# Two of the four weight chunks of the first layer's output product as groups of seven products of sums

## The chip, the cores and the metric

The kernel runs on one core of a Trainium2 chip. The metric is the time of one launch on the device in microseconds (us), the median of several runs. The core has five engines that run side by side, each with its own queue: TensorE (PE in the profile; its weight loads stand apart as PEld), VectorE (DVE), ScalarE (ACT), GpSimd (POOL) and SyncE (SP, which here only starts transfers). They wait for each other by semaphores.

## What is computed

A block of two layers over 528 tokens (16 meta tokens and 512 of the input) with 1024 channels, all in float32. What matters here is how a layer ends and how the next begins:

```python
def hybrid_layer(x, norm_g, w_in, ..., w_a, w_b, w_out, cos, sin, k_top):
    h = rms_norm(x, norm_g)
    proj = jnp.einsum('btd,de->bte', h, w_in)
    ...
    y_a = jnp.einsum('bte,ed->btd', attn * jax.nn.silu(gate_a), w_a)
    ...
    y_b = jnp.einsum('bte,ed->btd', pooled * jax.nn.silu(gate_b), w_b)
    g_a, g_b = jnp.split(jax.nn.sigmoid(merge), 2, axis=-1)
    return x + jnp.einsum('btd,de->bte', g_a * y_a + g_b * y_b, w_out)
```

The last line is the output product: a 528 x 1024 matrix of merged activations by the 1024 x 1024 matrix `w_out`. Its result is the next layer's input `x`, and the next layer starts with the sum of squares over the channels of each token (`rms_norm`).

## The kernel before

**Precision.** TensorE takes its operands as `F32R` (a rounded float32). To keep more digits, every operand is split into a high part (a cast by ACT) and a rest (value minus high part, a subtraction by DVE or POOL), and a product is made in three passes that accumulate in one PSUM bank: high by high, high by rest, rest by high. Activations lie transposed: channels in the 128 partitions (eight blocks, index `k` or `j`), tokens along the free axis.

**Weights.** `chunks` lists pieces of the weight matrices in the order of use, 27 per layer; the last four of a layer are 256 columns of `w_out` each (numbers 23 to 26 in the first layer), and before them stand the two chunks of `w_a` (21, 22). SP loads a chunk into two `raw` buffers; four such buffers are there, two chunks at a time, and `w_load` starts the next load where a chunk's buffers come free. The splitting is cut into items in `prep_q`; `group_done`, called after every group of matmuls, runs one item. There are three kinds. Plain chunks: two casts of 1024 elements by ACT and two subtractions by DVE. Chunks in `by_dma`: the rest is made by ACT (minus the value, rounded) and a transfer from POOL's queue that adds the value onto it, so that DVE has nothing to do; then the two casts. Chunks in `mixed`: see below.

**Groups of seven products.** `group_of_products` multiplies a chunk of 256 columns, seen as 2 x 2 blocks (input channels halved, output channels halved), by activations seen as 2 x 2 blocks (channels halved, tokens halved), with seven block products in place of eight. `mixed_prep` makes the seven left operands of a chunk in nine items (four blocks and three sums `s1`, `s2`, `s3`/`s4` of blocks, each with a high part and a rest; two of the sums are made by accumulating transfers on POOL's queue, `first_sum` and the one from `s2` onto `a12`). The seven right operands are four sums and three plain blocks. Each product is 12 matmuls. Three PSUM banks serve a group; `out` copies a bank to a sheet (ACT), `total` adds a bank and a sheet (DVE), `direct` takes a bank. Before the change the groups serve the ten `mixed` chunks of `w_in` in each layer (`mix_gates`), and the last two chunks of `w_out` in the second layer only (`mix_out`, with right operands from `sums_of_merged`).

**The end of the first layer.** Chunks 21 and 22 (`w_a`) are multiplied in eight channel blocks `j`, each in two token parts (272 and 256 tokens) of 12 matmuls. After each part DVE finishes `ta[j]` with two instructions, ACT casts it to `hhi`, and POOL makes the rest `hlo` (DVE does for `j` = 7). Then `out_group` makes one block of 128 output channels for one token part: 24 matmuls of a dense product, one DVE instruction that adds half the result to the residual `RES`, ACT's square, and POOL's addition of the square to `sq`. Chunks 23 and 24 run over both token parts. Chunks 25 and 26 are held together: first both for tokens 0 to 271, then both for tokens 272 to 527. Between the second token part's four blocks stand `stats(0)` (sums of squares of the first token part, on TensorE) and `norm_half(1, 0, ...)` (its normalization for the second layer). The second layer begins with `plain_trio`, which reads `NF[0]` of the first token part, block after block.

**Order.** PE and DVE follow the order of the code. ACT, POOL and SP are put in order by the framework's scheduler; `issue_after` sets a lower bound for some. `later(fn, n)` runs `fn` n groups later; `group_done` calls `half_done`, and `dense` also calls one of them halfway through a block.

The names the steps below use: `chunks`, `mixed`, `by_dma`, `SOFT`, `first_sum`, `mixed_prep` (items `i0` to `i8`), `half_done`, `group_of_products`, `ROLES`, `NEEDS`, `LEAD`, `sums_of_merged`, `out_group`, `stats`, `norm_half`.

## Time and profile before

| | us |
|---|---|
| median of 3 runs (735.25 to 736.46) | 735.64 |
| the profiled execution | 736.32 |
| its span, first to last instruction | 734.5 |
| chunks 21 and 22 (`w_a`, first layer) | from about 305.9 to 329.3 |
| output product of the first layer | 329.3 to 378.0 |

The span is split by the profile into instructions of each engine. A matmul's end is modelled and matmuls overlap, so the pitch, the distance from one start to the next, is what a matmul costs; the durations (near 0.28 us) are longer than the pitch. "Idle before" an instruction names who ended the wait. A busy PE is therefore read from gaps and pitches, not from the busy share. Every line that the argument uses is shown in the prediction.

### The profile page before, as it was taken

How to read it: one execution, taken by the hardware profiler on the slowest of the kernel's cores; microseconds unless marked ns; L12 is line 12 of the kernel's file. 1: busy time of each engine (PE TensorE's matmuls, PEld its weight loads, DVE VectorE, ACT ScalarE, POOL GpSimd, SP SyncE). 2: the span in 40 equal slices, each digit the busy share in tenths (PEclk: the TensorE clock that was granted, in tenths of full speed). 3: DMA queues.
4: the chain of work that ended last, by engine and by line, in shares of the span. 5: the costliest groups of instructions: out<-in, count | busy, mean ns of one | idle time of the engine just before them, and what ended most of it. 6: DMA issues, size and time to landing. Idle time of an engine off the chain costs nothing.

```text
span 734.5 us, 16031 instructions
## 1 busy us (share of the span) xinstructions
PE 726.9 (99%) x5917; PEld 701.1 (95%) x5917; DVE 589.4 (80%) x1480; ACT 487.2 (66%) x1109; POOL 254.6 (35%) x337
## 2 busy tenths in 40 slices
PE   8999999999999999999999999999999999999998
PEld 8999999999999999999999989999899999999997
DVE  6776899999997776794358668999989978668774
ACT  6669735766789887543245696357588978775643
POOL 3652174731221211173247421757132222106300
PEclk9999999999999999999999999999999999999999
DMA  8766675874564434633422678649565654447832
GB/s 268 234 172 155 164 159 116 216 160 101 119 141 115 90 87 113 209 125 126 136 89 87 172 170 203 159 116 200 131 153 107 143 113 93 114 140 237 202 88 72
DMA packets 103566, 106.41 MB, mean 145 GB/s; under 512 B 5008, under 2 KB 83632, under 8 KB 103488
## 3 DMA queue, kind: packets, MB, share of 16 engines
q1 hardware_dynamic: 91888, 74.89, 33.4%
q0 software_dynamic: 11520, 30.41, 23.3%
q8 instruction: 46, 0.75, 0.4%
q14 instruction: 32, 0.26, 0.1%
q10 hardware_dynamic: 80, 0.08, 0.0%
HBM read 66.41 MB, written 8.55 MB: 102 GB/s over the span
## 4 chain that ended last, share of the span: by engine, by line
PE 90%; DVE 4%; DMA 2%; ACT 2%; issue 1%; POOL 1%; SPq 1%; DVEq 0%; POOLq 0%; ACTq 0%
PE d L63 73%; PE a L63 12%; PE v L63 4%; DMA xt<-in_x_dram 2%; DVE w L63 1%; DVE alo L63 0%; SPq L156 0%; DVE c L63 0%; SPq L434 0%; DVE sila L63 0%; ACT w L225 0%; DVE t L63 0%; ACT w L269 0%; POOL t L683 0%; ACT lt L800 0%
## 5 line engine op out<-in xcount | busy, mean ns | idle before, releaser
L63 PE MATMUL d<-hhi,w 128*128 128x256 f32 (+3 forms) x1392 | 278.8, 291 | 0.3 <-DVE c L63 0.3
L63 PEld LDWEIGHTS d<-hhi,w 128*128 128x128 f32 x1392 | 222.2, 188 | 3.8 <-DVE c L63 0.7
L63 PE MATMUL d<-hlo,w 128*128 128x256 f32 (+3 forms) x696 | 189.8, 288 | 0.0
L63 DVE TENSOR_TENSOR w<-raw,w 128x512 fp32r<-128x512 f32 (+1 forms) x156 | 122.6, 792 | 15.5 <-ACT w L269 14.9
L63 PEld LDWEIGHTS d<-hlo,w 128*128 128x128 f32 x696 | 131.3, 189 | 1.5 <-issue 0.2
L63 PE MATMUL d<-hsum,w 128*128 128x264 f32 (+1 forms) x720 | 95.1, 285 | 0.1
L63 PEld LDWEIGHTS d<-hsum,w 128*128 128x128 f32 x720 | 89.7, 188 | 0.9 <-issue 0.3
L63 PE MATMUL d<-w,hhi 128*128 128x256 f32 x576 | 86.3, 287 | 0.1
L269 ACT CAST w<-raw 128x512 fp32r<-128x512 f32 x132 | 79.0, 624 | 5.2 <-DMA raw<-s 4.3
L63 PEld LDWEIGHTS d<-w,hhi 128*128 128x128 f32 x576 | 74.7, 188 | 5.0 <-issue 2.8
L255 POOL DMA_DIRECT2D raw<-raw x22 | 19.8, 902 | 106.1 <-DVE w L63 22.1
L63 DVE MATCH_REPLACE8 sc<-m,sc 128x400 f32<-128x400 f32 (+2 forms) x100 | 54.3, 546 | 0.0
L63 DVE MAX8 m<-sc 128x8 f32<-128x400 f32 (+2 forms) x100 | 53.3, 556 | 0.9
L221 POOL DMA_DIRECT2D w<-raw x34 | 31.7, 948 | 64.1 <-ACT w L220 44.6
L284 POOL DMA_DIRECT2D raw<-s x22 | 19.3, 876 | 87.8 <-DVE s L63 40.7
L800 ACT ACTIVATE lt<-lt,mn,NR 128x144 f32<-128x144 f32 (+3 forms) x64 | 42.3, 663 | 11.2 <-DVE mn L63 10.5
L63 DVE SCALAR_TENSOR_TENSOR sc<-r,wsg,sc 128x144 f32<-128x144 f32 (+3 forms) x56 | 32.4, 582 | 16.9 <-ACT r L720 14.5
L63 PE MATMUL d<-w,hlo 128*128 128x256 f32 x288 | 45.6, 281 | 0.0
L63 PE MATMUL d<-mhi,w 128*128 128x272 f32 (+2 forms) x192 | 45.5, 324 | 0.0
L815 POOL TENSOR_SCALAR pm<-lt,rs 128x16 f32<-128x16 f32 x48 | 26.6, 583 | 50.2 <-DVE rs L63 38.6
L1446 POOL TENSOR_TENSOR hlo<-ta,hhi 128x256 fp32r<-128x256 f32 (+1 forms) x28 | 27.0, 975 | 41.6 <-ACT hhi L1444 27.7
L683 POOL TENSOR_TENSOR t<-t,t 128x256 f32<-128x256 f32 (+1 forms) x34 | 32.3, 949 | 25.7 <-DVE t L63 24.3
(253 smaller groups left out, 1564.2 us busy)
## 6 DMA issues: line engine op xcount, KB each, us to landing
raw<-in_w_in_dram SPq DMA_DIRECT2D x88, 256.0 KB, 3.4
w<-raw POOLq DMA_DIRECT2D x34, 512.0 KB, 5.8
raw<-in_w_in_dram SPq DMA_DIRECT2D x32, 512.0 KB, 4.5
raw<-in_w_out_dram SPq DMA_DIRECT2D x12, 512.0 KB, 3.4
raw<-raw POOLq DMA_DIRECT2D x22, 256.0 KB, 4.0
raw<-s POOLq DMA_DIRECT2D x22, 256.0 KB, 3.5
kept<-res SPq DMA_DIRECT2D x16, 264.0 KB, 3.1
res<-kept SPq DMA_DIRECT2D x16, 264.0 KB, 5.9
```

The lines of the kernel that those rows point to most:

```text
L63: return fn(*a, **k)
L221: gp.dma_start(t, raws[c][s], accum_op=OP.add)
L255: gp.dma_start(raws[c][0][:, 1], raws[c][0][:, 0], accum_op=OP.add)
L269: act.copy(t[:, 0], blk[src[n]])
L284: gp.dma_start(blk["a12"], blk["s2"], accum_op=OP.add)
L683: added[0] = gp.tensor_tensor(t1[:m, :256], t1[:m, :256], t2[:m, :256], op=OP.add).ins
L800: act.activation(L[hh][:, :n], L[hh][:, :n], AF.Exp, scale=NR[:, i, h:h + 1], bias=mn[:, hh:hh + 1], accum_out=sm[:, hh:hh + 1])
L815: (gp if j < 3 else dve).tensor_scalar(pms[i][:, 2 * j + hh, :], L[hh][:, 0:16], rs[:, hh:hh + 1], None, op0=OP.mult)
L1446: pool_end = gp.tensor_sub(hlo[:, j, a:a + n], d, f(hhi[:, j, a:a + n]))
```

## The change

The four `w_out` chunks of the first layer are treated in three ways. Chunk 23 stays a dense product over both token parts, but its weights are split as a `by_dma` chunk. Chunks 24 and 25 become `mixed` and are multiplied by `group_of_products`, with tokens halved at 264. Chunk 26 stays a dense product, with its two blocks first for tokens 0 to 271, then for tokens 272 to 527. `sums_of_first` makes the four sums of the merged activations in place in `ta`, their high parts and their rests: ten instructions of the sums at set places in chunk 22 (`OWHEN`), of which six stand behind its last block, the casts and rests of three sums in `trickle`, from which every `half_done` now takes two entries, and the rests of these three on POOL (`OPOOL`). `SOFT` lets the rest of block `a12` of chunk 24 be made by ACT and an accumulating transfer in place of DVE. `stats(0)` and `norm_half(1, 0, ...)` now also come from `trickle`: half a block and one block after the first token part of chunk 26.

```diff
+SOFT = {-3: ("a12",), -2: ()}
+OWHEN = {0: (((0, 1), 0),), 1: (((2, 3), 0),), 2: (((0,), 1), ((0,), 2)), 3: (((1,), 1), ((1,), 2), ((2, 3), 1), ((2, 3), 2))}
+OPOOL = (2, 3, 4)
+SOFT_A = (0,)
...
+        if l == 0:
+            mixed |= {len(chunks) + 1, len(chunks) + 2}
+            by_dma |= {len(chunks) - i for i in SOFT_A}
         chunks += [[(w_rows(w_out[l], c, 256), 0)] for c in (0, 256, 512, 768)]
...
         def lo(n):
-            dve.tensor_sub(ops[n][:, 1], blk[src[n]], f(ops[n][:, 0]))
+            if n in SOFT.get(c - len(chunks) // 2, ()):
+                with marked():
+                    act.activation(ops[n][:, 1], blk[src[n]], AF.Copy, scale=-1.0)
+                gp.dma_start(ops[n][:, 1], blk[src[n]], accum_op=OP.add)
+            else:
+                dve.tensor_sub(ops[n][:, 1], blk[src[n]], f(ops[n][:, 0]))
...
+    trickle = deque()
+
     def half_done():
+        for _ in range(2):
+            if trickle:
+                trickle.popleft()()
...
+    def sums_of_first(ta, n2):
+
+        c0, c1 = slice(0, n2), slice(n2, 2 * n2)
+        t1 = one.tile([128, 2, 4, n2], F32R, tag="D", name="osum1")
+        own = {}
+
+        def sums(ks, part):
+            for k in ks:
+                a0, a1, b0, b1 = ta[k][:, c0], ta[k][:, c1], ta[4 + k][:, c0], ta[4 + k][:, c1]
+                if part == 0:
+                    dve.tensor_tensor(a0, a0, a1, op=OP.subtract)
+                    act.copy(t1[:, 0, k], a0)
+                elif part == 1:
+                    dve.tensor_tensor(a1, b1, a1, op=OP.subtract)
+                elif part == 2:
+                    dve.scalar_tensor_tensor(b1, b1, -1.0, a0, op0=OP.mult, op1=OP.subtract)
+                else:
+                    dve.scalar_tensor_tensor(b0, b1, -1.0, b0, op0=OP.mult, op1=OP.subtract)
+
+        src = {2: lambda k: ta[4 + k][:, c1], 3: lambda k: ta[k][:, c1], 4: lambda k: ta[4 + k][:, c0]}
+
+        def high(n, k):
+            if n not in own:
+                own[n] = one.tile([128, 2, 4, n2], F32R, tag={2: "Ahi", 3: "Alo", 4: "C"}[n], name=f"osum{n}")
+            if n == 4 and k in (0, 2):
+                sums((k, k + 1), 3)
+            act.copy(own[n][:, 0, k], src[n](k))
+
+        def low(n, k):
+            (gp if n in OPOOL else dve).tensor_sub(own[n][:, 1, k], src[n](k), f(own[n][:, 0, k]))
+
+        def low1(k):
+            dve.tensor_sub(t1[:, 1, k], ta[k][:, c0], f(t1[:, 0, k]))
+
+        items = deque()
+        for n in (2, 3, 4):
+            for k in range(4):
+                if True:
+                    items.append(lambda n=n, k=k: (high(n, k), later(lambda: low(n, k), 1)))
...
+                if l == 0 and c:
+                    for ks, part in OWHEN.get(mi, ()):
+                        osums(ks, part)
+                        if part == 0:
+                            for k in ks:
+                                later(lambda k=k: low1(k), 1)
...
-            for c in range(2):
-                w = chunk()
+            trickle.extend(oitems)
+            w = chunk()
+            for mi in range(2):
+                out_group(w, mi, mi, halves)
+            while trickle:
+                trickle.popleft()()
+            base = popped[0] - progress[W["use"]]
+            for q in range(2):
+                def add(eh, t, src):
+                    j = 2 + 2 * q + eh
+                    cs = slice(t * n2, (t + 1) * n2)
+                    d = RES[0][:, j, cs]
+                    dve.scalar_tensor_tensor(d, src, -0.5 if eh else 0.5, d, op0=OP.mult, op1=OP.add)
+                    squares(j, cs, d)
...
+                group_of_products(q, base, n2, operands, total, add)
+            flush_prep()
+            w = chunk(ahead=False)
+            for hs in (halves[:1], halves[1:]):
                 for mi in range(2):
-                    out_group(w, mi, 2 * c + mi, halves)
-            w2 = chunk()
-            flush_prep()
-            w3 = chunk(ahead=False)
-            for hs in (halves[:1], halves[1:]):
-                for c, w in ((2, w2), (3, w3)):
-                    for mi in range(2):
-                        out_group(w, mi, 2 * c + mi, hs)
-                    if c == 2 and hs[0][0] == 1:
-                        w_prep_enqueue()
+                    out_group(w, mi, 6 + mi, hs)
                 if hs[0][0] == 0:
-                    later(lambda: stats(0), 1)
-                    later(lambda: norm_half(1, 0, mm, LAG2), 2)
+                    w_prep_enqueue()
+                    trickle.extend((lambda: None, lambda: stats(0), lambda: None,
+                                    lambda: norm_half(1, 0, mm, LAG2)))
```

More of the change, by code (lines that the diff above doesn't have):

```diff
@@ L212, in low @@
                 w_load()
+                first_sum(c + 1)
         def second():
@@ L1105, in mix_gates @@
                 later(lambda: SIL.update(ready=True), 4)
+    def sums_of_first(ta, n2):
[30 more added lines that the diff above has]
+                    items.append(lambda n=n, k=k: (high(n, k), later(lambda: low(n, k), 1)))
+        operands = {
+            "a11": lambda s, k: H[s][:, k, c0],
+            "a12": lambda s, k: H[s][:, 4 + k, c0],
+            "s4": lambda s, k: H[s][:, 4 + k, c1],
+            "s1": lambda s, k: t1[:, s, k],
+            "s2": lambda s, k: own[2][:, s, k],
+            "s3": lambda s, k: own[3][:, s, k],
+            "a22": lambda s, k: own[4][:, s, k],
+        }
+        return sums, items, low1, operands
     def sums_of_merged(ta):
@@ L1434, in tile_block @@
             w = chunk()
+            if l == 0 and c:
+                osums, oitems, low1, operands = sums_of_first(ta, n2)
             if l and c:
@@ L1451, in tile_block @@
                         group_done()
+                if l == 0 and c:
+                    for ks, part in OWHEN.get(mi, ()):
[3 more added lines that the diff above has]
+                                later(lambda k=k: low1(k), 1)
                 if c == 0:
@@ L1463, in tile_block, with squares @@
             dve.memset(mm, 1.0)
+            def squares(j, cs, d):
+                n = cs.stop - cs.start
+                t = tmp.tile([128, HB], F32, tag="tt", name="tq", bufs=6)
+                act.activation(t[:, :n], d, AF.Square, scale=D ** -0.5)
+                gp.tensor_tensor(sq[:, cs], sq[:, cs], t[:, :n], op=OP.add)
             def out_group(w, mi, j, halves):
@@ L1492, in stats, with total @@
                 inv_rms(mm[:, c], None)
-            for c in range(2):
-                w = chunk()
-                for mi in range(2):
-                    out_group(w, mi, 2 * c + mi, halves)
-            w2 = chunk()
-            flush_prep()
-            w3 = chunk(ahead=False)
-            for hs in (halves[:1], halves[1:]):
-                for c, w in ((2, w2), (3, w3)):
-                    for mi in range(2):
-                        out_group(w, mi, 2 * c + mi, hs)
-                    if c == 2 and hs[0][0] == 1:
-                        w_prep_enqueue()
+            trickle.extend(oitems)
[12 more added lines that the diff above has]
+                    squares(j, cs, d)
+                def total(eh, t, ps, part):
+                    o = sheet(n2, "c")[:, :n2]
+                    dve.tensor_tensor(o, ps[:, :n2], part, op=OP.add)
+                    add(eh, t, o)
+                group_of_products(q, base, n2, operands, total, add)
+            flush_prep()
+            w = chunk(ahead=False)
+            for hs in (halves[:1], halves[1:]):
+                for mi in range(2):
+                    out_group(w, mi, 6 + mi, hs)
                 if hs[0][0] == 0:
-                    later(lambda: stats(0), 1)
-                    later(lambda: norm_half(1, 0, mm, LAG2), 2)
+                    w_prep_enqueue()
+                    trickle.extend((lambda: None, lambda: stats(0), lambda: None,
+                                    lambda: norm_half(1, 0, mm, LAG2)))
             hooks = {0: lambda: stats(1), 1: lambda hf: None if hf else norm_half(1, 1, mm, LAG3)}
```

## The prediction

> **What bounds the kernel now.** I read the page first: the engines' busy shares, then the chain that ended last.
>
> ```profile
> PE 726.9 (99%) x5917; PEld 701.1 (95%) x5917; DVE 589.4 (80%) x1480; ACT 487.2 (66%) x1109; POOL 254.6 (35%) x337
> PE 90%; DVE 4%; DMA 2%; ACT 2%; issue 1%; POOL 1%; SPq 1%; DVEq 0%; POOLq 0%; ACTq 0%
> ```
>
> TensorE sets the end. An average over the whole span says little about this stage, so next comes the chain in order of time around the first layer's output product (start, length, what):
>
> ```profile
> 304.35 63.54 PE d L63 x516
> 367.88 1.17 PE a L63 x12
> 369.05 2.93 PE d L63 x24
> 371.98 0.52 PE a L63 x3
> 372.50 11.08 PE d L63 x80
> ```
>
> From 304.35 to beyond 378 the chain is nothing but matmuls: whatever TensorE no longer does here is a gain, and whatever it newly waits for is a loss, one for one. The busy time of each engine in the stretches of this stage shows who has room:
>
> ```profile
> 318.00:329.26 11.26, 11.26 (x95) 11.26 (x94) 10.61 (x18) 4.82 (x11) 7.63 (x9) 1.00 0.28 93
> 329.26:341.00 11.74, 11.74 (x97) 11.63 (x96) 7.15 (x13) 4.66 (x8) 4.64 (x5) 1.00 0.34 114
> 341.00:353.00 12.00, 12.00 (x101) 12.00 (x100) 4.00 (x6) 4.13 (x7) 3.79 (x4) 1.00 0.41 136
> 353.00:367.88 14.88, 14.88 (x123) 14.75 (x122) 4.91 (x7) 2.66 (x6) 3.40 (x4) 1.00 0.42 123
> ```
>
> The columns are length, PE, PEld, DVE, ACT, POOL (busy us and instructions), granted clock, DMA share, GB/s. The clock is 1.00 throughout. In the first stretch (chunk 22) DVE is busy 10.61 of 11.26 us: it is nearly a second bound. In the output product it is busy a third to 60% of the time: there is room for more sums.
>
> **The change, part by part.** *Matmuls.* The end of a block is seen in the DVE instruction that reads its bank:
>
> ```profile
> 344.34 0.44 DVE L63 SCALAR_TENSOR_TENSOR res<-d,res 128x272 f32<-128x272 f32 x1 [2.59 <-PE d L63]
> 347.18 0.42 DVE L63 SCALAR_TENSOR_TENSOR res<-d,res 128x256 f32<-128x256 f32 x1 [2.40 <-PE d L63]
> 350.19 0.44 DVE L63 SCALAR_TENSOR_TENSOR res<-d,res 128x272 f32<-128x272 f32 x1 [1.45 <-PE d L63]
> ```
>
> A block of 24 matmuls takes 347.18 - 344.34 = 2.84 us at 256 tokens and 350.19 - 347.18 = 3.01 us at 272, so 0.118 and 0.125 us for one, in proportion to the columns; 264 columns lie midway, 0.122. A dense chunk is two blocks of each kind, 11.70 us. A group of seven products is 7 x 12 x 0.122 = 10.24 us. Two chunks save 2 x 1.46 = **2.92 us**. That products keep this pace is seen where the second layer's output already has them:
>
> ```profile
> 708.63 2.68 PEld L63 LDWEIGHTS d<-osum,w 128*128 128x128 f32 x22 [0.34 <-DVE w L63]
> 719.71 3.01 PE L63 MATMUL d<-osum,w 128*128 128x256 f32 x24
> 722.57 0.38 PE L63 MATMUL a<-consts,res 128*128 128x128 f32 x2
> ```
>
> Two products of 256 columns: 722.57 - 719.71 = 2.86 us for 24 matmuls, 0.119 each. The same stretch lost 0.34 us once, to a weight rest that DVE made late. `stats` (1.17 us) and the transposes (0.52) stay.
>
> *Entry into the output product.* Its first block reads `hlo` of block 7, which DVE makes last:
>
> ```profile
> 324.44 1.80 DVE L63 TENSOR_TENSOR w<-raw,w 128x1024 fp32r<-128x1024 f32 x1
> 327.84 1.80 DVE L63 TENSOR_TENSOR w<-raw,w 128x1024 fp32r<-128x1024 f32 x1
> 329.57 0.42 DVE L63 SCALAR_TENSOR_TENSOR ta<-ta,d 128x272 f32<-128x272 f32 x1
> 331.03 0.99 DVE L63 TENSOR_TENSOR hlo<-ta,hhi 128x272 fp32r<-128x272 f32 x1 [0.49 <-ACT hhi L1444]
> 332.08 0.39 PE L63 MATMUL d<-hlo,w 128*128 128x272 f32 x1
> 333.51 0.43 DVE L63 TENSOR_TENSOR hlo<-ta,hhi 128x256 fp32r<-128x256 f32 x1 [0.47 <-ACT hhi L1444]
> 334.20 0.29 PE L63 MATMUL d<-hlo,w 128*128 128x256 f32 x1
> ```
>
> The rest is ready at 332.02 and TensorE takes it at 332.08: no slack at all; for the second token part 0.26 us (333.94 to 334.20). Before these, the change removes two weight rests (3.6 us as they ran) and adds ten instructions: four sums, their four rests `low1`, two more sums. The nearest rows are the second layer's sums:
>
> ```profile
> L63 DVE TENSOR_TENSOR ta<-ta x8: 415/418/421, 687.2 to 696.1; 128x256 f32<-128x256 f32 x8
> 689.99 1.09 DVE L63 TENSOR_TENSOR osum<-ta,osum 128x256 fp32r<-128x256 f32 x3
> L1446 POOL TENSOR_TENSOR hlo<-ta,hhi x9: 735/937/1719, 316.7 to 328.5; 128x256 fp32r<-128x256 f32 x5, 128x272 fp32r<-128x272 f32 x4
> ```
>
> Back to back they come each 0.36 us (1.09 / 3): ten are 3.7 us, as much as goes. Beside a busy POOL a DVE instruction with two SBUF inputs is longer: the same `hlo` took 0.99 us with POOL at work and 0.43 without. POOL has 7.63 us in this stretch and gets two DMA issues of 0.88 more (row below). So DVE comes between 0.2 us earlier and 2 us later to block 7; I take 0.4 later, the removed pair having run at contended length and some of the ten doing so too. **Loss 0.4 us (-0.2 to 2.0).** The six sums behind block 7 (2.2 us) delay the first `res` instruction to about 337; its bank is needed again only by the fourth block, at about 338, so they cost nothing. If that cover goes, TensorE waits for the bank.
>
> Chunk 23's weights now come by transfer. Their buffers are free when chunk 21 is done, halfway through 305.9 to 329.3, near 318; a rest lands 5.8 us after its issue, and the issue takes POOL 0.88 us:
>
> ```profile
> w<-raw POOLq DMA_DIRECT2D x34, 512.0 KB, 5.8
> raw<-raw POOLq DMA_DIRECT2D x22, 256.0 KB, 4.0
> L284 POOL DMA_DIRECT2D raw<-s x22 | 19.3, 876 | 87.8 <-DVE s L63 40.7
> ```
>
> So with the casts at 318 to 321 (two of about 1 us) the second rest lands near 328, before its use at about 332: nothing. The new loads from SP change shape, not bytes, and each chunk's load still has the whole of a chunk in front of it: nothing; a late one would show as TensorE waiting for a cast.
>
> *The two groups.* DVE, in the 10.2 us of the first group: five rests of chunk 24, and of chunk 25 two sums and three rests (ten of 0.6 us back to back, from the 0.68 us row below) and seven instructions of about 0.43 for totals and residuals: 9 us. It fits with 1 us to spare. ACT gets 15 weight instructions of 512 elements (0.62 us, row below) and 18 casts and bank copies of about half the size, and loses four casts of twice the size: at 0.62 each for all that comes, and 1.24 for what goes, at most 15.5 us more in 38.6, of which 27 are free. POOL is the tight one. It issues five transfers more (0.88 each) and makes twelve rests, all due before the last product of the first group:
>
> ```profile
> L63 DVE TENSOR_TENSOR w<-raw,w x12: 681/685/693, 699.8 to 722.2; 128x512 fp32r<-128x512 f32 x12
> L269 ACT CAST w<-raw 128x512 fp32r<-128x512 f32 x132 | 79.0, 624 | 5.2 <-DMA raw<-s 4.3 <-DVE raw L63 0.8
> 331.69 1.07 POOL L488 TENSOR_TENSOR Sg<-consts,gk 128x320 f32<-128x320 f32 x1
> 369.38 0.88 POOL L496 TENSOR_TENSOR msq<-msq,mhalf 128x3 f32<-128x3 f32 x1 [5.43 <-DVE msq L63]
> 370.25 0.74 POOL L1474 TENSOR_TENSOR sqs<-sqs,tq 128x256 f32<-128x256 f32 x1
> ```
>
> POOL ends its old work (`tables`, last row 331.69 + 1.07) at about 333 to 335, with the two DMA issues of chunk 23 ahead. Most sums are ready from 335.5. Eleven rests at 0.74 to 0.94 (least and median of the row above), three additions of squares at 0.74 to 1.0 (stretched in the same measure) and three issues at 0.88 are 13 to 16 us: done at 348.5 to 351.5. TensorE begins the last product at 329.26 + 11.7 + 6 x 1.46 + 0.4 = 350.1 and needs the last rest 1.1 us later, at 351.2. POOL is not bound to the order of the code: the square root's power (369.38) ran ahead of the square's addition (370.25), which the code issues first. **Loss 0.5 us (0 to 5)**, near the lower end because the two sums nearly meet; the row beside it is the 0.34 us above.
>
> [...]
>
> *Boundary to the second layer.* `stats(0)` had a whole block (2.84 us) between the last block it reads and itself, now half (1.42); the normalization had two blocks ahead of `plain_trio`, now one.
>
> ```profile
> 365.08 0.44 DVE L63 SCALAR_TENSOR_TENSOR res<-d,res 128x272 f32<-128x272 f32 x1 [2.57 <-PE d L63]
> 365.61 0.43 ACT L1477 ACTIVATE tl<-res 128x272 f32<-128x272 f32 x1 [2.57 <-DVE res L63]
> 372.54 1.73 DVE L63 SCALAR_TENSOR_TENSOR nf<-res,parT,a 128x272 f32<-128x272 f32 x4
> 376.15 0.89 DVE L63 SCALAR_TENSOR_TENSOR nf<-res,parT,a 128x272 f32<-128x272 f32 x2
> 378.01 5.58 PE L63 MATMUL d<-raw,nf 128*128 128x200 f32 x32
> ```
>
> The last square ends 366.04 - 365.08 = 0.96 us after its block: inside 1.42. The power ends at 370.26, 1.21 us after `stats` (369.05): inside the other half block. `NF` is complete at 377.04, 4.5 us after the transposes; the trio now starts 2.84 us after them but takes its eight blocks 0.70 us apart (5.58 / 8), the last 2.84 + 4.9 = 7.7 us after: covered. **Loss 0.1 us (0 to 1.7)**, the upper end if `NF` had to be complete before the trio starts (4.5 - 2.84).
>
> *Sum.* -2.92 + 0.4 + 0.5 + 0.1 = -1.9 us. The profiled execution took 736.32 us (span 734.5, 1.8 around it): it would take 734.4. That execution lies 0.7 above the median of 735.64, so for the median I write 735.64 - 1.9 = **733.7 us**.
>
> **The rivals.** *The exclusion of DVE and POOL eats the gain.* In the 22 us from 329.3 to 351.2 stand about 20 DVE instructions with two SBUF inputs (ten sums, ten rests and sums of weights: 10 x 0.36 + 10 x 0.6 = 9.6 us) and POOL's twelve rests, squares and tables (9 + 3 + 2.5 = 14.5 us at uncontended length). If they cannot run together they need 24.1 us, so the last product starts 2 us late; with 0.4 at the entry, -2.92 + 2.4 = -0.5: 735.1. For it: the 0.99 us. Against it: part of DVE's work reads PSUM, and some may fall where POOL issues transfers. [...]
>
> *Slower: POOL's queue stands behind a transfer.* The rest of `a12` now lands by a transfer, and only then may the next transfer, `s2` onto `a12`, be issued. If the scheduler has put it ahead of the rests, POOL stands for the landing, 4.0 us, with the rests behind it: last rest at 353.5 to 356. TensorE loses one for one from 351.2 on; from 354.1 on the 2.92 are gone. At 356 and with the 0.4 at the entry: -2.92 + 4.8 + 0.4 = +2.3: 737.9. For it: the scheduler works with guessed durations. Against it: the cast and the transfer need only raw weights and a buffer free at 329.3, so the transfer can land before DVE has made `s2` (about 338).
>
> *The whole saving.* Chunk 22's DVE work gets shorter, POOL keeps up: -2.9, 732.7.
>
> *The pace of products.* If a matmul's pitch were set by its weight load, fewer columns would save nothing, and nothing would change (735.6). The pitches 0.118 and 0.125 speak against it.
>
> **How the numbers follow.** A measurement here can tell about 0.2%, 1.5 us, from no change: faster is below 734.2, slower above 737.1. Forecast (losses 0.5 to 1.5): 0.42; whole saving (losses below 0.5): 0.18; exclusion (losses 1.5 to 4.4): 0.27; POOL behind a transfer: 0.11; pace: 0.02. Faster 0.60, same 0.30 (with the pace and a little of the transfer case), slower 0.10. The range goes from the whole saving with 0.3 of scatter, 732.4, up into the slower case, 736.6; the likeliest case alone is 733.2 to 734.2.
>
> **What would show it.** Right: TensorE's products of chunks 24 and 25 start about 10.3 us apart, the trio starts 1.5 to 2.9 us earlier than 378.0, and all that lies behind it is shifted by the same. Entry: PE idle near 332 released by DVE `hlo`. Groups: PE idle at `osum` released by POOL `osum` (rests late) or by DVE `w` (weight rests late); in the slower case POOL has a gap of some us that ends with a DMA. Boundary: idle before the `ones` matmuls or before the trio. The forecast is wrong if these gaps sum to over 1.5 us, or if the second layer, which the change doesn't touch, does not simply move along.

## The result

The changed kernel takes 741.93 us in the median of six runs (741.32 to 742.43), the kernel before 735.45 (735.03 to 736.46) on the same chip: a ratio of 1.0085, with a 95% interval of 1.0072 to 1.0098. The prediction was 733.7 us, with a range up to 736.6. The sign was wrong, and the time was off by 8 us. In the six sessions of this document the kernel before had medians from 735.45 to 737.13 us, and in the twenty profiles the output product starts between 328.1 and 330.4 us, a difference that is there already at 302 us, ahead of chunk 21; so beside each ratio stands the length of the stage itself.

The page of the changed kernel, its busy times and its chain:

```profile
PE 728.1 (98%) x5893; PEld 700.3 (95%) x5893; DVE 609.9 (82%) x1517; ACT 500.5 (68%) x1144; POOL 270.8 (37%) x356
PE 77%; DVE 14%; ACT 3%; DMA 2%; issue 2%; SPq 1%; POOL 1%; DVEq 0%; ACTq 0%; POOLq 0%
```

TensorE has 24 instructions fewer, as counted, and yet its share of the chain falls from 90% to 77%, while VectorE's rises from 4% to 14%. So the matmuls went, and the chain runs through VectorE more often; how much TensorE waits is read from its gaps. The windows of the same four stretches as before (length, PE, PEld, DVE, ACT, POOL, clock, DMA share, GB/s):

```profile
318.00:329.26 11.26, 11.26 (x95) 11.26 (x94) 10.74 (x25) 7.81 (x17) 6.39 (x8) 1.00 0.87 206
329.26:341.00 11.74, 9.57 (x62) 8.93 (x61) 10.44 (x15) 4.89 (x12) 11.48 (x14) 0.85 0.48 95
341.00:353.00 12.00, 11.08 (x91) 10.87 (x91) 11.51 (x19) 7.05 (x18) 9.85 (x11) 1.00 0.24 68
353.00:367.88 14.88, 14.57 (x120) 14.37 (x120) 13.37 (x23) 10.08 (x20) 6.80 (x7) 1.00 0.69 196
```

From 329 to 341 us TensorE gets through 62 matmuls where the kernel before made 97. GpSimd is busy for 11.48 of 11.74 us, VectorE for 10.44 (before: 4.64 and 7.15). The granted clock is 0.85. TensorE's timeline names the waits (start, length, what, idle before and who ended it):

```profile
329.62 0.29 PE L67 MATMUL d<-hlo,w 128*128 128x272 f32 x1
...
331.85 0.39 PE L67 MATMUL d<-hlo,w 128*128 128x272 f32 x1 [0.56 <-POOL hlo L1517]
334.16 0.39 PE L67 MATMUL d<-hhi,w 128*128 128x272 f32 x1 [1.04 <-ACT hhi L1515]
335.11 0.39 PE L67 MATMUL d<-hlo,w 128*128 128x272 f32 x1 [0.56 <-DVE hlo L67]
335.59 0.28 PE L67 MATMUL d<-hlo,w 128*128 128x256 f32 x1
...
336.18 0.28 PE L67 MATMUL d<-hhi,w 128*128 128x256 f32 x1
336.30 0.28 PE L67 MATMUL d<-hlo,w 128*128 128x256 f32 x1
...
337.42 0.41 PE L67 MATMUL d<-hlo,w 128*128 128x256 f32 x1
337.64 0.41 PE L67 MATMUL d<-hhi,w 128*128 128x256 f32 x1
...
339.95 0.29 PE L67 MATMUL d<-hlo,w 128*128 128x272 f32 x1
...
345.80 0.28 PE L67 MATMUL d<-hlo,w 128*128 128x264 f32 x1
...
349.66 4.66 PE L67 MATMUL d<-osum,w 128*128 128x264 f32 x36 [0.92 <-ACT p L1059]
357.79 0.39 PE L67 MATMUL d<-hhi,w 128*128 128x264 f32 x1 [0.30 <-DVE w L67]
...
381.33 1.85 PE L67 MATMUL d<-raw,nf 128*128 128x200 f32 x10
```

At 336.3 a matmul of 256 columns follows the one before it after 0.12 us, at 337.64 after 0.22 (337.64 - 337.42): the clock is about halved, from 336.4 to 339.95, 3.5 us (the granted clock of 336.42 to 339.95 is 0.52). Three waits of at most 1.04 us, 2.2 in all, came before the fall. The rows at 329.62, 335.59, 339.95 and 345.80 are the second matmuls of chunk 23's first, second and third block and of the first product. The first block, with the waits, took 5.97 us, the second, with the halved clock, 4.36, and the last two 5.85; at the prediction's pace they take 3.01, 2.84 and 5.85. (One of the six runs had a mean granted clock of 1.000, so hardly such a fall, and took 742.30 us, no less than the others: what the fall costs in the end is not told by the times.)

What GpSimd and VectorE did at that place, two timelines:

```profile
329.43 0.88 POOL L263 DMA_DIRECT2D raw<-raw  x1 [3.67 <-DMA raw<-in_w_out_dram]
330.05 2.42 POOL L1517 TENSOR_TENSOR hlo<-ta,hhi 128x256 fp32r<-128x256 f32 x3
```

```profile
329.31 0.43 DVE L67 TENSOR_TENSOR ta<-ta 128x264 f32<-128x264 f32 x1
329.84 2.93 DVE L67 SCALAR_TENSOR_TENSOR ta<-ta 128x264 f32<-128x264 f32 x1
332.69 0.42 DVE L67 SCALAR_TENSOR_TENSOR ta<-ta,d 128x272 f32<-128x272 f32 x1
```

Two things are to be seen. GpSimd stood for 3.67 us at the transfer `first_sum(25)`, which waits for a load, with three rests `hlo` behind it. And a sum of 264 columns, 0.43 us of work, took VectorE 2.93 us (329.84 to 332.77), beside three rests that GpSimd made back to back (330.05 to 332.47); the instruction behind it begins the finish of block 7, for which TensorE waits, at 332.69 where the kernel before has it at 329.57.

Where the time went, by three marks of TensorE in each profile: the output product's first matmul, the second layer's first (`raw,nf`), and the end of the span.

| kernel | output product to second layer | second layer's first matmul to the end | ratio to before (95%) |
|---|---|---|---|
| before | 378.01 - 329.26 = 48.75 | 734.5 - 378.01 = 356.5 | 1 |
| changed | 381.33 - 329.49 = 51.84 | 740.3 - 381.33 = 359.0 | 1.0085 (1.0072 to 1.0098) |

Of the 5.8 us of span, 0.2 lie ahead of the output product, 3.1 in it, and 2.5 in the second layer, which the change does not touch. The 3.1 are the 2.92 saved and 6.0 lost.

### The profile page after: what moved, and what is told of

It reads as the page before. It is cut to its first block, busy times and chain, and to the rows that moved or that the text cites. A ratio compares the mean times of both kernels' runs of the same rounds, so it can differ in the third digit from the quotient of the medians.

```text
span 740.3 us, 16101 instructions
## 1 busy us (share of the span) xinstructions
PE 728.1 (98%) x5893; PEld 700.3 (95%) x5893; DVE 609.9 (82%) x1517; ACT 500.5 (68%) x1144; POOL 270.8 (37%) x356
## 4 chain that ended last, share of the span: by engine, by line
PE 77%; DVE 14%; ACT 3%; DMA 2%; issue 2%; SPq 1%; POOL 1%; DVEq 0%; ACTq 0%; POOLq 0%
PE d L67 63%; PE a L67 11%; DVE w L67 4%; PE v L67 3%; DVE ta L67 2%; DMA xt<-in_x_dram 2%; DVE s L67 1%; DVE lt L67 1%; DVE t L67 1%; DVE c L67 1%; ACT w L277 1%; DVE hlo L67 1%; DMA raw<-s 1%; DVE sc L67 1%; DVE sila L67 1%
## 5 line engine op out<-in xcount | busy, mean ns | idle before, releaser
L67 PE MATMUL d<-hhi,w 128*128 128x256 f32 (+3 forms) x1312 | 266.7, 293 | 2.5 <-ACT hhi L1515 1.0
L67 PEld LDWEIGHTS d<-hhi,w 128*128 128x128 f32 x1312 | 211.3, 190 | 6.8 <-DVE w L67 1.7
L67 PE MATMUL d<-hlo,w 128*128 128x256 f32 (+3 forms) x656 | 181.4, 290 | 1.1 <-POOL hlo L1517 0.6
L67 PEld LDWEIGHTS d<-hlo,w 128*128 128x128 f32 x656 | 124.3, 190 | 3.0 <-POOL hlo L1517 0.8
L277 ACT CAST w<-raw 128x512 fp32r<-128x512 f32 x144 | 85.9, 622 | 6.5 <-DMA raw<-s 4.6
L263 POOL DMA_DIRECT2D raw<-raw x24 | 22.1, 923 | 119.7 <-DMA raw<-in_w_in_dram 20.7
L229 POOL DMA_DIRECT2D w<-raw x36 | 33.4, 942 | 65.3 <-ACT w L228 45.1
L297 POOL DMA_DIRECT2D raw<-s x24 | 21.0, 875 | 83.3 <-DVE s L67 32.8
L833 POOL TENSOR_SCALAR pm<-lt,rs 128x16 f32<-128x16 f32 x48 | 28.7, 621 | 46.2 <-DVE rs L67 39.8
L228 ACT ACTIVATE w<-raw 128x1024 fp32r<-128x1024 f32 x36 | 37.6, 1058 | 4.1 <-PE d L67 4.1
```

Of the source, the lines that this page charges most:

```text
L67: return fn(*a, **k)
L228: act.activation(t, raws[c][s], AF.Copy, scale=-1.0)
L229: gp.dma_start(t, raws[c][s], accum_op=OP.add)
L263: gp.dma_start(raws[c][0][:, 1], raws[c][0][:, 0], accum_op=OP.add)
L277: act.copy(t[:, 0], blk[src[n]])
L297: gp.dma_start(blk["a12"], blk["s2"], accum_op=OP.add)
```

## The experiments

Every ratio is to the kernel before on the same chip, in the same session; between sessions that kernel moved by as much as many of the differences, so ratios of two sessions are compared with care. "First layer" is the first of the two columns above, "second layer" the second.

**The transfer in GpSimd's queue.** `first_sum(25)` may not be issued before the last rest `hlo`; nothing else moves.

```diff
-            first_sum(c + 1)
+            with tc.issue_after(added[0]) if c == len(chunks) // 2 - 3 else nullcontext():
+                first_sum(c + 1)
```

> The changed kernel with one POOL instruction moved: the accumulating transfer that makes chunk 25's first weight sum is queued behind the last rest hlo of chunk 22 instead of ahead of three of them. All other queues are in the same order as in the changed kernel. Theory A (that transfer, which waits for a load, holds up three rests, and the waits and the slower TensorE clock near 330 to 346 follow from it): the dense chunk 23 takes 11.7 to 12.5 us instead of 16.3, the wait for the bank copy p1 (1.1 us) shrinks, and the time is 735.5 to 737.5. Rival (VectorE is overloaded by the sums by itself, the transfer is only where it shows): chunk 23 stays above 14.5 us and the time above 740.

Measured: 740.47 us, ratio 1.0073 (1.0057 to 1.009); first layer 51.35. The wait for GpSimd's `hlo` is gone, but TensorE waits nearly as long elsewhere, 1.8 us in place of 2.2:

```profile
333.00 0.40 PE L67 MATMUL d<-hhi,w 128*128 128x272 f32 x1 [1.62 <-ACT hhi L1516]
```

So the stall of the queue is real, but it is worth about 0.5 us (first layer, 51.84 to 51.35), not 5; the intervals of the two ratios overlap. The profiled span is 1.6 us shorter, but 0.9 of that lie ahead of the output product. Chunk 23 still takes 15.56 us (the same count gave 16.18), and the time is above 740: both are the signs of the rival. VectorE is late at block 7 with or without the stall.

**The second layer.** The steps of the index and attention work are dealt out by a counter, `credit`, of which `half_done` adds a part at each call and keeps the fraction. The change calls `half_done` twice less in the first layer, so that the second starts from 0.9 and not from 0.1. One kernel sets the changed kernel's counter back, another sets the kernel before to 0.9:

```diff
+        if l:
+            credit[0] = 0.1
```

> The changed kernel with one number of its planner set at the start of the second layer to what it is in the kernel before: credit 0.1 in place of 0.9. Credit sets after which half block of matmuls a step of the second layer's index and attention work is put in. Theory B (the 2.4 us lost in the second layer come from that other interleaving): the second layer, from its first product to the end, is 1.8 to 2.6 us shorter, time 739.3 to 740.3. Rival (they come from the later or busier start of that layer): time within 0.7 of 741.9.

> The kernel before, with credit set to 0.9 at the start of the second layer and nothing else changed. Theory B: 1.8 to 2.6 us slower than before, 737.2 to 738.1, all of it in the second layer. Rival: 735.0 to 736.0, no change.

Measured: the changed kernel with 0.1 takes 739.77 us, ratio 1.0051 (1.0038 to 1.0064), the interval below that of the changed kernel; second layer 738.2 - 381.32 = 356.9. The kernel before with 0.9 takes 737.2, ratio 1.0021 (1.0012 to 1.003), 1.55 us more in the median, though its profile shows only 0.6 us of this (735.1 - 378.03 = 357.1). Two windows of the second layer, the changed kernel first, then with 0.1:

```profile
581.33:606.33 25.00, 24.48 (x215) 23.73 (x214) 19.12 (x55) 19.90 (x49) 6.40 (x9) 1.00 0.54 113
631.33:656.33 25.00, 24.38 (x219) 23.63 (x218) 17.80 (x49) 19.70 (x45) 4.32 (x7) 1.00 0.41 96
```

```profile
581.32:606.32 25.00, 25.00 (x224) 24.65 (x223) 20.27 (x57) 20.71 (x51) 6.13 (x9) 1.00 0.61 137
631.32:656.32 25.00, 25.00 (x228) 24.52 (x229) 19.38 (x50) 19.50 (x44) 3.17 (x5) 1.00 0.41 97
```

TensorE has idle time there, 1.1 us in these two windows, that is gone with 0.1; the matmuls of the second layer then come in the same order as in the kernel before. In the changed kernel the counter is worth 2.1 us (359.0 to 356.9). The two other profiles of a changed kernel that keeps 0.9 have 358.8 and 358.7 us, and all those with 0.1 lie between 356.6 and 357.2. In the kernel before it is worth less, 0.6 to 1.6 us; why is open.

**Both together.** 

> Both edits together. Theories A and B with the saving of 2.92 us in the matmuls: 733.0 to 735.0, a little faster than the kernel before. If either falls, 736 to 740.

Measured: 738.72 us, ratio 1.0046 (1.0031 to 1.006), outside the expected range by 3.7 us. First layer 52.84, second 357.0. Two waits stand in the first layer: 1.60 us for `hhi` of block 7, and 1.75 for a bank copy of the first group, with the clock down behind it (0.86 from 341 to 353 us). ScalarE's timeline shows why the copy is late:

```profile
347.06 0.42 ACT L1559 ACTIVATE tq<-res 128x256 f32<-128x256 f32 x1 [1.11 <-DVE res L67]
347.38 0.36 ACT L1060 COPY p<-d 128x264 f32<-128x264 f32 x1
```

The bank was ready; the copy stood in the queue behind a square that waited for VectorE. The next four edits start from this kernel.

**VectorE's sums ahead of block 7; the square.** Three edits: the four instructions (two rests, two sums) that VectorE makes between its rows of blocks 6 and 7 go behind block 7; the last square of chunk 23 goes behind the copy; both.

```diff
-OWHEN = {..., 2: (((0,), 1), ((0,), 2)), 3: (((1,), 1), ((1,), 2), ...)}
+OWHEN = {..., 3: (((0,), 1), ((0,), 2), ((1,), 1), ((1,), 2), ...)}
...
-                                later(lambda k=k: low1(k), 1)
+                                later(lambda k=k: low1(k), 1 + k // 2)
```

```diff
+                    elif j == hf == 1:
+                        later(lambda a=a, n=n, d=d: squares(1, slice(a, a + n), d), 2)
```

> The kernel with the sum of chunk 25 moved and the planner's credit set back (738.7 us), and besides the sums of the quarters that VectorE makes between the rows before block 7 of the gate product (the rests of the quarter sums for k 2 and 3, and second and third sums for k 0; some 2.9 us of VectorE with the stretching) now stand behind block 7. Theory A (VectorE's new sums ahead of block 7 make TensorE wait 1.8 us there, and the clock falls after that for about another 1.5 us): the wait for hhi goes, the granted clock of 329 to 341 us returns to 1.00, and the time is 735.5 to 736.5. Rival B (VectorE has too much to do over the whole stretch from 318 to 353 us, so what leaves block 7 comes back at the first product's bank copy or at the second group): 737.5 to 739.

> The same base (738.7 us), and the square of chunk 23's last block on ScalarE is issued behind the bank copy of the first product instead of ahead of it. Theory A (the copy p1 waits 1.75 us only because it stands in ScalarE's queue behind a square that waits for VectorE; the clock falls after that wait): the wait goes, and the time is 735.5 to 737. Rival B (the products only reach VectorE's late sums sooner, and wait there): 738 to 739. Block 7's wait stays in both.

> Both edits together on the same base (738.7 us): the sums behind block 7, and the last square behind the first bank copy. If both theories hold: 732.5 to 734.5, that is the kernel before less about what its removed products cost. If VectorE's load over the whole stretch is the bound: 736 to 739.

Measured: sums behind block 7, ratio 1.0057 (1.0034 to 1.0079), no gain; square later, 1.0034 (1.0021 to 1.0047), first layer 51.18; both, 1.0043 (1.0026 to 1.006). With the sums behind block 7 the wait there is gone and a longer one comes, for a bank that VectorE's residual has not yet read:

```profile
342.50 0.39 PE L67 MATMUL d<-hhi,w 128*128 128x256 f32 x1 [3.07 <-DVE res L67]
```

The two kernels with this wait differ in what the clock makes of it. From 341 to 353 us, the sums alone and then with the square:

```profile
341.00:353.00 12.00, 8.79 (x70) 8.57 (x71) 11.51 (x19) 7.25 (x17) 10.44 (x11) 1.00 0.24 68
```

```profile
341.00:353.00 12.00, 10.40 (x71) 10.19 (x72) 11.80 (x19) 7.36 (x17) 10.46 (x11) 0.86 0.25 68
```

The same wait (3.07 and 3.04 us) left the clock at 1.00 in one, and it is 0.86 in the other: the fall is not a fixed price of a wait. What decides it, no run here shows.

At this point rival B, that VectorE has too much to do, looked right: the times of all three, 740.97, 738.54 and 739.99 us, lie in its ranges or above. The next runs tell VectorE's load from what GpSimd does to it.

**GpSimd's tables.** The second layer's tables are made much earlier in GpSimd's queue: without the lower bound of `issue_after` the scheduler puts the two large operations at 148 and 150 us; before, they ran from 330.9 to 333.8.

```diff
-            with tc.issue_after(pool_end.ins):
-                tables(1, True)
...
+            tables(1, True)
             flush_prep()
```

> The same base (738.7 us), and the second layer's three table operations of GpSimd (4.8 us of its time between 330 and 334 us, beside VectorE's block 7) are made much earlier, elsewhere in GpSimd's queue. [...] Rival A (VectorE is late by its own sums): the wait stays above 1.2 us and the time is 738 to 739.5.

Measured: 738.41 us, ratio 1.0019 (1.001 to 1.0028) against 1.0046. Most of the fall of the ratio comes from the kernel before, which had 735.65 us in the earlier session and 737.04 in this one; the medians of the two edited kernels, 738.72 and 738.41, hardly differ, and 738.41 lies where rival A put it. The profile tells more: the wait for `hhi` falls from 1.60 to 1.00, below the 1.2 of rival A and above the 0.6 (with a time of 736 to 737.5 us) that was expected if GpSimd is what makes VectorE late, and the first layer from 52.84 to 51.40, though VectorE's order of work is the same. So GpSimd has a part in VectorE's lateness.

**Rests and sums.** From the kernel with the later square (1.0034): the twelve rests of the quarter sums on VectorE, the sixteen sums left out, the twelve rests left out, and the earlier tables (the edit above).

```diff
-OPOOL = (2, 3, 4)
+OPOOL = ()
```

```diff
                 if part == 0:
-                    dve.tensor_tensor(a0, a0, a1, op=OP.subtract)
                     act.copy(t1[:, 0, k], a0)
-                elif part == 1:
...
-                    dve.scalar_tensor_tensor(b0, b1, -1.0, b0, op0=OP.mult, op1=OP.subtract)
```

```diff
-                    items.append(lambda n=n, k=k: (high(n, k), later(lambda: low(n, k), 1)))
+                    items.append(lambda n=n, k=k: high(n, k))
...
-            "s2": lambda s, k: own[2][:, s, k],
+            "s2": lambda s, k: own[2][:, 0, k],
...
```

> Base: the kernel with the sum of chunk 25 moved, the credit set back and the last square behind the first bank copy (ratio 1.0034 to the kernel before). The twelve rests of the quarter sums are made by VectorE instead of GpSimd. Theory E (exclusion: while GpSimd makes rests, a pair of VectorE's sums takes 1.7 to 1.9 us instead of 0.77): each pair after 333 us is back at 0.8, and since the twelve rests cost VectorE only some 4.6 us of its own, about what the stretching took, the ratio stays or falls: 0.998 to 1.004. Rival L (VectorE's load by count decides, the stretching is small change): 4.6 us more of VectorE in the stretch from 330 to 350 us, of which most comes out behind TensorE: ratio 1.006 to 1.010.

> Same base (ratio 1.0034). The sixteen VectorE operations that make the quarter sums are left out (what is multiplied are the quarters as they stand); their casts, their rests and all products stay. Theory L (VectorE has more to do between 318 and 353 us than there is time, and the sums are what is too much): no wait over 0.5 us is left on TensorE between 328 and 358 us, the granted clock stays 1.00, and the ratio is 0.995 to 0.999, about the prediction's sum. Rival E (GpSimd's work shuts VectorE out whatever VectorE has to do): block 7 keeps a wait of about a microsecond, ratio 1.000 to 1.003.

> Same base (ratio 1.0034). GpSimd's twelve rests of the quarter sums are left out (the products take the rounded part in their place); VectorE's order of instructions is the same to the last one. Theory E: VectorE's pairs of sums behind block 7 fall from 1.9 to 0.8 us, the wait at the second group (1.1 us) goes, block 7's wait (1.6 us) shrinks little, because what stretches VectorE there are the tables and the transfers' issues; ratio 1.000 to 1.002. Rival L (the load alone): ratio 1.003 to 1.004, no change.

> Same base (ratio 1.0034) and the second layer's tables made earlier (that alone gave 1.0019 against 1.0046). If the two gains add: ratio 1.0005 to 1.0015. If the wait only moves on to the next of VectorE's late results: 1.002 to 1.003. Below 0.998 on either theory would mean that VectorE catches up once GpSimd leaves it alone at block 7.

| kernel | ratio (95%) | first layer, us |
|---|---|---|
| rests on VectorE | 1.0019 (1.0009 to 1.0028) | 50.05 |
| no sums on VectorE | 1.0056 (1.0038 to 1.0074) | 50.48 |
| no rests on GpSimd | 1.0007 (0.9996 to 1.0019) | 48.48 |
| tables earlier | 1.0013 (1.0003 to 1.0023) | 49.75 |

The base has 51.18 us in the first layer. Twelve instructions *more* on VectorE and none of these on GpSimd made it 1.1 us shorter; the intervals of the two ratios overlap a little. The twelve rests left out, with VectorE's order the same, made it 2.7 us shorter, with the waits as theory E had them: the one at block 7 stays (1.61 us), the one at the second group (1.09) is gone. That the transfers' issues stretch VectorE, as that expectation has it, is not shown: in the changed kernel the sum at 337.99 us took 0.43 inside an issue that ran from 337.54 to 338.43. The earlier tables made it 1.4 us shorter, as much as without the later square. The clock is luck in this comparison: with the same wait of 1.6 us at block 7 it is 0.85 from 329 to 341 us in the kernel with the rests on VectorE and 1.00 in the base and without the rests. Sixteen instructions *less* on VectorE gained 0.7 us in the profile and nothing in the ratio, which lies outside both expectations; its profiled run, 737.77 us, was its fastest, and the other four took 740.2 to 741.2. VectorE's timeline without the sums, and GpSimd's beside it:

```profile
329.16 0.44 DVE L67 TENSOR_TENSOR ta<-ta,zb 128x272 f32<-128x272 f32 x1
330.09 4.03 DVE L67 TENSOR_TENSOR hlo<-ta,hhi 128x272 fp32r<-128x272 f32 x1 [0.48 <-ACT hhi L1511]
334.04 0.41 DVE L67 SCALAR_TENSOR_TENSOR ta<-ta,d 128x256 f32<-128x256 f32 x1
```

```profile
330.01 1.58 POOL L506 TENSOR_TENSOR Cg<-consts,gk 128x320 f32<-128x320 f32 x1
330.86 1.54 POOL L507 TENSOR_TENSOR Sg<-consts,gk 128x320 f32<-128x320 f32 x1
331.69 3.02 POOL L1148 TENSOR_TENSOR osum<-ta,osum 128x264 fp32r<-128x264 f32 x3
```

One rest of 0.44 us took 4.03 (330.09 to 334.12), beside five GpSimd instructions without a gap; TensorE waited 2.52 us for it. (Without the sums the casts run earlier, so GpSimd's rests stand closer: the edit moved the collision rather than taking it away, and what the sums cost by themselves is not told by it.) With the rests left out, VectorE's pairs of sums behind block 7 are these:

```profile
337.26 0.77 DVE L67 TENSOR_TENSOR ta<-ta 128x264 f32<-128x264 f32 x2
337.95 0.77 DVE L67 SCALAR_TENSOR_TENSOR ta<-ta 128x264 f32<-128x264 f32 x2
```

With the rests on GpSimd, in the base of this run, the same two pairs took 1.34 and 1.90 us:

```profile
336.55 1.34 DVE L67 TENSOR_TENSOR ta<-ta 128x264 f32<-128x264 f32 x2
337.80 1.90 DVE L67 SCALAR_TENSOR_TENSOR ta<-ta 128x264 f32<-128x264 f32 x2
```

So GpSimd's work stretches VectorE's, and that costs time. It does not follow that VectorE's load costs nothing; the next runs show that it does.

**Both reliefs of GpSimd.** On the kernel with the later square; then with the sums behind block 7 as well; then on the changed kernel alone; and the tables alone on the kernel before.

> Base: the kernel with the sum of chunk 25 moved, the credit set back and the last square behind the first bank copy (ratio 1.0034). Both reliefs of GpSimd together: the rests of the quarter sums on VectorE (alone 1.0019) and the second layer's tables earlier (with the same base 1.0013). Theory E (exclusion): no VectorE pair behind 330 us takes over 1.0 us, the wait at the second group and the fall of the clock go, and the ratio is 0.998 to 1.000. Rival L (VectorE's load by count): 1.001 to 1.003.

> The kernel with both reliefs of GpSimd (expected 0.998 to 1.000), and VectorE's sums taken from ahead of block 7 to behind it. With GpSimd busy that move lost: 1.0057 against 1.0046, with a new wait of 3.1 us for a bank behind the sums. Theory E: behind block 7 the sums now take 0.4 us each instead of 0.95, VectorE gets to the residual in time, neither wait is left, and the ratio is 0.995 to 0.998, near the prediction's 0.9975. Rival L: twenty operations and twelve rests of 0.4 us are 12 us of VectorE in the 11.7 us of chunk 23, the wait for a bank comes back with 1 to 3 us, ratio 1.000 to 1.004.

> The changed kernel as it is (1.0085), with both reliefs of GpSimd and nothing else: the rests of the quarter sums on VectorE, the tables earlier. The sum of chunk 25 still stands ahead of three rests in GpSimd's queue, the planner's credit and the square are as changed. [...]

> The kernel before, with the tables made earlier and nothing else. [...] Below 0.998 would mean that the tables' move is a gain of its own, which the comparisons with the kernel before must then be cleared of.

Measured: 1.0003 (0.9992 to 1.0013), first layer 49.70; with the sums behind block 7, 0.9999 (0.9986 to 1.0012), first layer 48.59; the changed kernel with both reliefs alone, 1.0047 (1.003 to 1.0065) against 1.0085, where 1.0035 to 1.0055 was expected if GpSimd's stretching of VectorE is the largest part of the loss and 1.007 to 1.0085 if it is a small one; the control, 0.9979 (0.997 to 0.9988), below the 0.9990 to 1.0005 expected of it, first layer 48.60. GpSimd's relief alone takes 2.8 us off the changed kernel by the ratios, 1.8 by the medians and 1.0 in the profile's first layer (50.83); that profile also lacks the halved clock, which cost 1.5, so its worth there is not settled. And the sums behind block 7, which had lost with a busy GpSimd, now cost no wait there: VectorE reaches the first residual at 335.32 us, in time as the prediction had thought (about 337), because each sum takes 0.43 again:

```profile
333.05 0.43 DVE L67 TENSOR_TENSOR ta<-ta 128x264 f32<-128x264 f32 x1
333.58 0.43 DVE L67 SCALAR_TENSOR_TENSOR ta<-ta 128x264 f32<-128x264 f32 x1
333.94 0.77 DVE L67 TENSOR_TENSOR ta<-ta 128x264 f32<-128x264 f32 x2
334.62 0.77 DVE L67 SCALAR_TENSOR_TENSOR ta<-ta 128x264 f32<-128x264 f32 x2
335.32 0.43 DVE L67 SCALAR_TENSOR_TENSOR res<-d,res 128x272 f32<-128x272 f32 x1
```

Chunk 23 (from second matmul to second matmul) shows that both edits were needed; the transfer, the counter and the square are as repaired in all four:

| chunk 23, us | sums ahead of block 7 | sums behind it |
|---|---|---|
| GpSimd busy | 14.83 | 16.53, of which about 1.5 for the clock |
| GpSimd relieved | 13.33 | 11.70, as a dense chunk should |

What is left is a wait for a weight rest, in TensorE's timeline of that kernel:

```profile
345.50 4.38 PE L67 MATMUL d<-osum,w 128*128 128x264 f32 x34 [1.76 <-DVE w L67]
```

From the first residual to this wait's end VectorE has no idle time at all (third busy number):

```profile
335.32:345.50 10.18, 8.25 (x66) 7.83 (x65) 10.18 (x27) 6.03 (x15) 4.29 (x3) 1.00 0.30 81
```

This is the part of rival L that holds. Both kernels missed theory E's ranges (0.998 to 1.000 and 0.995 to 0.998): with most of the stretching gone, VectorE's own work, the twelve rests included, fills this stretch.

**The weights earlier, and the control again.** Two steps of the weight preparation are taken in the middle of chunk 23:

```diff
                 out_group(w, mi, mi, halves)
+                if mi == 0:
+                    prep_one()
+                    prep_one()
```

> The kernel with GpSimd relieved and the sums behind block 7 (0.9999), and two steps of the first group's weight preparation taken ahead, in the middle of chunk 23, so that the rest of the sum's weights stands ahead of the last residual and the last rests on VectorE. If that order was the cause of the 1.76 us: the wait falls under 0.4 us, from the output product's start to the second layer's first product it takes 47.0 to 47.4 us (48.6 before the move, 48.75 in the kernel before), and the ratio is 0.9970 to 0.9985. Rival (the next late result of VectorE, the last residual or the sums of the quarters, takes its place): a wait of a microsecond elsewhere on TensorE between 341 and 355 us, ratio 0.9990 to 1.0005.

> The kernel before with the tables made earlier, once more, beside the run above. Its first layer took 48.60 us from the output product's start to the second layer's first product, against 48.75: if the first 0.9979 was the chip's drift between runs, 0.9990 to 1.0003; if the tables' move is a gain of its own, 0.9970 to 0.9988.

Measured: 735.18 us, ratio 0.999 (0.9981 to 0.9999), first layer 47.66, the wait down to 1.09 and not under 0.4, so its order was only a part of the cause; the control 735.21 us, ratio 0.9989 (0.998 to 0.9998). The output product is now 1.1 us shorter than before. But the runs of this kernel reach from 734.3 to 736.5 us, and the profiled one (736.19) starts the output product 1.9 us later than the control's (330.16 against 328.29), with a wait of 1.1 us for `qs` early in the first layer that the control's profile does not have. From the output product's start to the end the two profiles take 404.2 and 404.9 us. So the two kernels cannot be told apart by their times, and with all these defects mended the regrouping has at most some 0.7 us over the kernel before with the tables moved, by one profile each. Whether moving the tables makes the kernel before faster is open: its medians, 735.38 and 735.21, are near those that the kernel before had in the first sessions (735.45 and 735.65), and its first layer is as long as before (48.60 and 48.59 against 48.75).

## Why the prediction was wrong

Of the 8.2 us between forecast and measurement some 4.1 are the entry, 1.0 the two groups and 2.5 the second layer, as the profile has them; the rest is the start of the profiled run and the boundary.

*Matmuls, -2.92 us: right.* 24 fewer, and the 36 matmuls of the row at 349.66 follow each other after 0.125 us ((4.66 - 0.28) / 35), near the 0.122 of the sum.

*Entry, loss 0.4 us (-0.2 to 2.0): this is the step that failed.* Chunk 23 took 345.80 - 329.62 = 16.18 us, not 11.70: a loss of 4.5. Counted from block to block, the three waits cost 3.0 (5.97 for 3.01) and the halved clock 1.5 (4.36 for 2.84). VectorE came to block 7 at 332.69 us, 3.1 later than the 329.57 of the kernel before. The text had the right rows (0.99 against 0.43 us for the same rest) and allowed at most 2.0, as if the exclusion could about double some of the instructions. The runs showed that an instruction of VectorE can take as long as a whole row of GpSimd's, 2.93 and 4.03 us for 0.43. It also counted the ten new instructions ahead of block 7 by the second layer's back-to-back row (689.99), where GpSimd computes nothing (8.45 us without an instruction up to 697.39), and had no term for the clock. (These ten are six sums and four rests; with the six behind block 7 there are twelve sums in chunk 22, not ten.) With GpSimd relieved and those sums ahead of block 7 a wait of 1.00 us stayed, and with the sums behind block 7 it went: so both the stretching and VectorE's own new work made the entry late.

*Chunk 23's weights: right; the loads, "nothing": wrong.* The second rest landed at 327.16 us, near the 328 of the forecast. But chunk 25's loads can start only when these transfers have read chunk 23's buffers, and `first_sum(25)` waits 3.67 us for one of them at the head of GpSimd's queue, with three rests `hlo` behind it. The text had looked for a late load at a cast, not in that queue. It cost about 0.5 us.

*The two groups, loss 0.5 us (0 to 5):* 1.5 measured. From the first product's second matmul to the second layer's first 381.33 - 345.80 = 35.53 us passed, 35.65 with the matmul ahead, against 20.48 for two groups, 11.70 for chunk 26 and the 1.95 that the kernel before has beside its four chunks. The engine named as the tight one was wrong: GpSimd's rests were in time; the bank copy behind a square (0.92) and a weight rest of VectorE (0.30, which the text did name) were late.

*Boundary, 0.1 us:* right; no wait stands before the trio.

*"All that lies behind it is shifted by the same": wrong*, by 2.5 us. The code was not touched there, but a counter runs through it, which is worth 2.1 of them.

*The rivals.* The exclusion named the right cause, GpSimd's work beside VectorE's, and was priced at 2.0 us by adding up uncontended lengths of two engines over the whole stretch; it struck at the entry instead, ahead of block 7. There single VectorE instructions with two SBUF inputs, 0.43 and 0.44 us by themselves, took 2.93 us in the changed kernel and 4.03 in the one without the sums, beside three and five GpSimd instructions in a row. Those with one input from PSUM did not stretch: `ta<-ta,d` and `res<-d,res` take 0.41 to 0.44 us in all these profiles. The slower rival, GpSimd's queue behind a transfer, came true with another transfer and other rests behind it; its own price would have been 4.8 us, the real one was about 0.5.

## What to carry over

Before moving work to GpSimd beside a busy VectorE, count VectorE's instructions with two SBUF inputs there as if they could last as long as GpSimd's uninterrupted row (here 2.93 and 4.03 us for 0.43 and 0.44, and 1.34 and 1.90 for pairs of 0.77), and ask which of them stands ahead of the critical one; here VectorE did twelve more instructions and the first layer became 1.1 us shorter. Then add up VectorE's own work as well: with GpSimd out of the way it was the next bound. When a wait on TensorE is expected to be paid "once", add the chance of half a clock for 3.5 us, 1.5 us here. And when code is rearranged, look for counters and planners that carry a state past the place: a fraction of a counter was worth 2 us in a layer that nobody touched.

## What the runs showed of the hardware that was not expected

A VectorE instruction with two SBUF inputs, 0.44 us by itself, took up to 4.03 us beside GpSimd instructions that started 0.7 to 0.9 us apart without a gap. Those with one input from PSUM kept their 0.41 to 0.44 us. TensorE's clock halved for 3.5 us after three waits of 2.2 us in all, and fell (0.86 from 341 to 353 us) after a single one of 3.04 us in one kernel, but not (1.00) after one of 3.07 in its neighbour; after a wait of 1.6 us for `hhi` of block 7 it was 0.85 from 329 to 341 us in two kernels and 1.00 in three others.
